# A hybrid decoder layer: all q, k, v projections as plain products ahead of the attention, without sums of x

## The chip, the core and the metric

The kernel runs on one core of one Trainium2 chip. The metric is device time in microseconds (us), the median of several executions. The engines named below are PE (matrix products; PEld is its weight load), DVE, ACT and POOL (element-wise work, each with its own instruction queue, worked off in order) and SP, whose queue issues nearly all DMAs of this kernel.

## What is computed

One decoder layer on x of 2048 rows by 1024 columns, in float32. The parts that matter here:

```python
h = rms_norm(x, g_mix)
z = h @ w_in                                  # 1024 x 3072
u, gb, gc, q, k, v = split(z, 6)              # 512 columns each
y_conv = gb * short_conv(gc * u, conv_w)      # causal, width 3, per channel
q = rms_norm(q per head of 64, g_q) / 8
k = rms_norm(k per head of 64, g_k)
y_attn = dilated_mixture(q, k, v)             # 8 heads, 3 branches (window, dilation)
mix = concat(rms_norm(y_conv), rms_norm(y_attn))
x = x + mix @ w_out
h = rms_norm(x, g_ffn)
x = x + (silu(h @ w_gate) * (h @ w_up)) @ w_down
```

## The kernel before, in words

Every float32 operand of a matrix product is split into a high and a low float16 half, and a product of two operands is three matmuls: high by high, high by low, low by high. The lines are those of the kernel shown at the end of this section. The class that runs is `Fast`; `General` is a fallback that the inputs don't call.

**Stages.** `in_and_conv` normalises x in 16 row tiles (`norm`), transposes them by DMA into `self.x[c]`, c = 0 to 3 with 512 rows each, and runs convolution tile 0 (128 of the 512 channels) on each of them as it arrives (`conv_steps(0, ...)`, matmuls at L191 to L193). Then come the projections: `project(g, c, W)` for four groups g of two heads and four row blocks c. One such call is called a unit in the prediction; there are 16. `attention_pairs` follows: 160 steps of attention (`attn_steps`), and between them steps of `fill`: convolution tiles 1 to 3 and the first part of the output projection, 356 steps. `RATE` is how many fill steps follow an attention step; 24 of them are placed ahead of the first. `out_b` is the rest of the output projection, `ffn` the feed-forward; neither is touched.

**A unit before.** A unit's product is done by Winograd's scheme in blocks of two by two: seven products instead of eight, each of 12 matmuls with 192 columns (L1237), in two halves t. Its left operands are x and four sums of blocks of x. `sums(c)` makes these: POOL adds the halves of x back together (L1134), DVE forms the sums (L1137 to L1140), ACT and DVE split them again (L1144, L1145). Its right operands are made by `operands(g)`: DVE finds the largest weight, ACT scales (L1163), POOL forms the sums (L1175 to L1182), and ACT and DVE split seven blocks (L1171, L1172). The products land in PSUM; ACT copies two of them out (L1247, L1254) and DVE adds the others (L1244). Then a chain follows: ACT squares q and k into the one buffer `row` (L1264) and splits v with DVE (L1267, L1268), DVE reduces (L1274), ACT takes a logarithm and an exponential, DVE does four small operations, POOL scales q and k (L1285) and applies the gain (L1290), ACT and POOL split them into the one buffer `qkhl` (L1294 to L1297), and SP writes it to `d_qk` in memory (L1298).

**Weights for later.** `spill_conv` and `spill_out` prepare the weights of convolution tiles 1 to 3 and of the output projection between the units, by the table `SPILLS`, and write them to memory. Their low halves are formed on DVE (L150, L1334).

**Order and buffers.** A scheduler puts the instructions on each engine's queue; `tc.issue_after(i)` places what follows behind instruction i on i's engine. The sums of x lie in the buffers `qT`, `ka` and `kb`, which the attention needs for q and the two halves of k: `load_pair` fills them by DMA transposes from `d_qk`. `regroup` rearranges q on POOL into `q16`. The attention's pools use the memory that the projection's pools (`tmp`, `fq`) leave.

Of the kernel before, what the change touches and what calls it, by code (L numbers as in the profile page):

```python
# [9 lines left out]
F32 = mybir.dt.float32  # L10
# [8 lines left out]
P = 128  # L19
# [7 lines left out]
HD = 64  # L27
# [983 lines left out]
class Fast(Builder):  # L1011
# [5 lines left out]
    RATE = 2.2  # L1017
# [16 lines left out]
    def in_and_conv(self):  # L1034
# [5 lines left out]
        with ExitStack() as c:  # L1040
# [11 lines left out]
            self.uc = cp.tile([P, 9], F32, name="uc")  # L1052
# [32 lines left out]
            ring = None  # L1085
            n = -1
            for step in self.conv_steps(0, W, before):
# [16 lines left out]
            for g in range(4):  # L1104
                Wg = Wn
                for i in range(4):
                    if g == 0 and i < 2:
                        self.sums(i + 2, s0)
                    if g < 3 and i == 1:
                        Wn = self.operands(g + 1)  # L1110
                    self.project(g, 3 - i if g == 3 else i, Wg)
                    if (g, i) == (0, 2):
                        self.g_out = self.gains(cp, [A["g_conv_out"][0], A["g_attn_out"][0]], "gout", 9)
                    for k in self.SPILLS.get((g, i), ()):
                        self.spill_conv(k // 3, k % 3) if k < 9 else self.spill_out((k - 9) // 2, (k - 9) % 2)
            self.st = dict()

    SPILLS = {(0, 3): (0,), (1, 0): (1, 2), (1, 2): (3,), (1, 3): (4,), (2, 0): (5, 6), (2, 2): (7,), (2, 3): (8,),
              (3, 0): (9, 10), (3, 1): (11, 12)}

    def sums(self, c, s0):
# [5 lines left out]
        Sc = self.sums_of[c] = [pool.tile([P, 2, 2, 4, 256], F16, name=name, bufs=2) for _ in range(2)]  # L1127
        xh, xl = self.x[c]
        for t in range(2):
            y = []  # L1130
            for i in range(2):
                o = slice((2 * t + i) * P, (2 * t + i + 1) * P)
                y.append(self.tmp.tile([P, KC, P], F32, name="t4"))
                nc.gpsimd.tensor_tensor(y[i], xh[:, :, o], xl[:, :, o], op=ALU.add)  # L1134
            a11, a12, a21, a22 = (y[i][:, 4 * k:4 * k + 4] for i in range(2) for k in range(2))
            v = nc.vector
            v.tensor_tensor(a22, a21, a22, op=ALU.add)  # L1137
            v.tensor_tensor(a21, a11, a21, op=ALU.subtract)
            v.tensor_tensor(a11, a22, a11, op=ALU.subtract)
            v.tensor_tensor(a12, a12, a11, op=ALU.subtract)  # L1140
            for i in range(2):
                src = y[i].rearrange("p (a k) t -> p a k t", a=2)
                hi, lo = (Sc[i][:, :, q, :, t * P:(t + 1) * P] for q in range(2))
                nc.scalar.copy(hi, src)  # L1144
                v.tensor_tensor(lo, src, hi, op=ALU.subtract)  # L1145

    def operands(self, g):
# [25 lines left out]
        p = nc.gpsimd  # L1173
        split(0, b11)
# [12 lines left out]
    def qk_constants(self):  # L1187
# [18 lines left out]
        self.vs = [self.fq.tile([P, 4, 2, 2, HD + 1], F16, name=f"vs{i}") for i in range(2)]  # L1206
# [4 lines left out]
    def project(self, g, c, W):  # L1211
# [8 lines left out]
        n = self.row.rearrange("p (j b d) -> p j b d", j=4, b=4)  # L1220
        F = []
        for t in range(2):
            pool, name = ((self.psmm, "mm"), (self.cvx, "cvx"))[self.units % 2]
            self.units += 1
            ps = [pool.tile([P, 512], F32, name=name)[:, 0:192] for _ in range(3)]

            def left(m, q, k):
                if m in (0, 1, 3):
                    i, k0 = {0: (2 * t, 0), 1: (2 * t, 4), 3: (2 * t + 1, 4)}[m]
                    return (xh, xl)[q][:, k0 + k, i * P:(i + 1) * P]  # L1230
                i, a = {5: (0, 0), 2: (0, 1), 6: (1, 0), 4: (1, 1)}[m]
                return Sc[i][:, a, q, k, t * P:(t + 1) * P]

            def product(m):
                for k in range(4):
                    for q, (x, y) in enumerate(((0, 0), (0, 1), (1, 0))):
                        nc.tensor.matmul(ps[self.BANK[m]], lhsT=left(m, x, k), rhs=W[m][:, y, k],  # L1237
                                         start=m in (0, 5, 4) and k == 0 and q == 0, stop=k == 3 and q == 2,
                                         skip_group_check=True)
            f = fq.tile([P, 2, 2, 192], F32, name="f", bufs=3)  # L1240
            F.append(f)

            def plus(o, bank, z):
                nc.vector.scalar_tensor_tensor(o, bank, u, z, op0=ALU.mult, op1=ALU.add)  # L1244
            f11, f12, f21, f22 = (f[:, i, h] for i in range(2) for h in range(2))
            product(0)
            nc.scalar.activation(f21, ps[0], AF.Copy, scale=u)  # L1247
            product(5)
            plus(f12, ps[1], f21)
            product(4)  # L1250
            if (g, c, t) == (0, 0, 0):
                self.squares(3, self.last, self.pstr.tile([P, 4], F32, name="tr"), False)
            product(1)
# [313 lines left out]
    def attention_pairs(self):  # L1567
# [9 lines left out]
        for _ in islice(fill, 24):  # L1577
            pass
# [315 lines left out]
```

## Time and profile before

| | us |
|---|---|
| median of 3 runs | 2207.26 (2206.59 to 2209.81) |
| the profiled execution | 2208.49 |
| its span | 2206.7 |
| PE busy | 2030.8 (92%) |
| DVE busy | 1526.2 (69%) |
| ACT busy | 1047.4 (47%) |
| POOL busy | 726.7 (33%) |
| mean granted TensorE clock | 0.963 |

The profile is of one execution; its own time stands beside its span. Times within it are us from the span's start unless marked ns. A line number is that of kernel and helper, so a helper's line collects all its callers. In the names, `mm`, `cvx`, `s` and `av` are PSUM tiles, `b` is x or a weight in transposed layout. A matmul's own duration overlaps the next one's: the distance of two starts tells the rate. The granted clock is a share of the full TensorE clock. What an engine waited for is inferred from semaphores.

### The profile page before, as it was taken

The numbers are of one execution on the slowest core, as the hardware profiler recorded it, in microseconds if no ns is written. First come the engines' busy times: TensorE is split into PE (matmuls) and PEld (weight loads), VectorE is DVE, ScalarE is ACT, GpSimd is POOL, SyncE is SP. The second block draws the span as 40 slices with busy tenths as digits, with TensorE's granted clock in tenths as the row PEclk, the third lists the DMA queues.
The fourth block names the chain that finished last, engine by engine and source line by source line (L and its number), as shares of the span: only waits on it lengthen the run. The fifth ranks groups of instructions, "written<-read, shape, count | busy, mean of one in ns | idle before, by whom it ended". The sixth has DMA issues, their size and how long they took to land.

```text
span 2206.7 us, 34303 instructions
## 1 busy us (share of the span) xinstructions
PE 2030.8 (92%) x12984; PEld 1115.8 (51%) x12984; DVE 1526.2 (69%) x2893; ACT 1047.4 (47%) x1967; POOL 726.7 (33%) x614
## 2 busy tenths in 40 slices
PE   3868778989999978998999999999999999999998
PEld 1347778946665653443444444444444444444443
DVE  7999885537776886687676666667676676545454
ACT  6445544447775766655333333334333244444341
POOL 2333434433433321122221112112222146555463
PEclk8879789999999998999999999999999999999999
DMA  9524454935867557799522332233222563251442
GB/s 240 138 84 138 158 154 130 192 74 148 180 136 193 167 140 200 244 248 293 161 101 91 101 115 82 91 107 113 90 95 102 210 243 123 77 178 53 130 139 87
DMA packets 460160, 317.00 MB, mean 144 GB/s; under 512 B 255568, under 2 KB 413264, under 8 KB 457808
## 3 DMA queue, kind: packets, MB, share of 16 engines
q1 hardware_dynamic: 442304, 291.56, 46.3%
q10 hardware_dynamic: 17680, 23.16, 2.9%
q8 instruction: 103, 1.69, 0.3%
q14 instruction: 73, 0.60, 0.1%
HBM read 157.96 MB, written 116.85 MB: 125 GB/s over the span
## 4 chain that ended last, share of the span: by engine, by line
PE 46%; issue 5%; DVE 4%; DMA 2%; SPq 2%; ACT 2%; POOL 1%; DVEq 0%; POOLq 0%; ACTq 0%
PE ps L812 28%; PE ps L945 15%; SPq L199 2%; DVE hl L680 1%; PE mm L191 1%; PE mm L192 1%; DVE w L933 1%; PE mm L193 1%; PE ps L191 1%; PE ps L192 0%; PE ps L193 0%; POOL x L952 0%; DMA b<-b 0%; ACT wq L742 0%; DMA wq<-d_a 0%
## 5 line engine op out<-in xcount | busy, mean ns | idle before, releaser
L812 PEld LDWEIGHTS <-w 128*128 128x128 f16 x3696 | 362.2, 98 | 448.0 <-issue 12.7
L812 PE MATMUL ps<-b,w 128*128 128x512 f16 x2112 | 464.8, 381 | 8.7 <-DMA b<-d_h 3.1
L945 PE MATMUL ps<-b,w 128*128 128x512 f16 x1848 | 399.7, 379 | 1.4 <-DVE s L966 0.8
L812 PE MATMUL ps<-hb,w 128*128 128x512 f16 x1584 | 347.1, 379 | 0.0
L945 PEld LDWEIGHTS <-w 128*128 128x128 f16 x1848 | 180.8, 98 | 220.1 <-issue 2.6
L705 POOL TENSOR_TENSOR t<-wq 128x512 f32<-128x512 f32 (+1 forms) x46 | 59.6, 1297 | 407.3 <-issue 231.1
L818 DVE TENSOR_TENSOR s<-ps,s 128x512 f32<-128x512 f32 x220 | 150.1, 683 | 37.1 <-PE ps L812 36.6
L952 POOL TENSOR_TENSOR x<-x,s 128x512 f32<-128x512 f32 x72 | 103.4, 1437 | 170.4 <-DVE s L966 133.1
L1511 DVE TENSOR_TENSOR et<-sm,et 128x512 f16<-128x512 f32 (+1 forms) x160 | 126.3, 807 | 41.8 <-ACT et L1510 40.8
L953 DVE SCALAR_TENSOR_TENSOR x<-ps,a_u,x 128x512 f32<-128x512 f32 x96 | 71.8, 749 | 101.7 <-PE ps L945 75.2
L1505 ACT ACTIVATE sm<-s,bound,kap 128x512 f32<-128x512 f32 (+1 forms) x160 | 116.6, 754 | 53.8 <-DVE s L1503 45.0
L191 PE MATMUL mm<-b,wq 128*128 128x512 f16 x320 | 125.7, 393 | 10.1 <-ACT cg L1360 8.6
L193 PE MATMUL mm<-b,wq 128*128 128x512 f16 x320 | 125.1, 391 | 3.4 <-DVE wq L150 3.4
L1237 PEld LDWEIGHTS <-b 128*128 128x128 f16 x1152 | 107.0, 105 | 40.1 <-issue 37.6
L192 PE MATMUL mm<-b,wq 128*128 128x512 f16 x320 | 125.1, 391 | 0.0
L722 ACT CAST w<-t 128x512 f16<-128x512 f32 x88 | 53.7, 616 | 129.2 <-PE ps L812 81.2
L1503 DVE TENSOR_TENSOR s<-s,mask 128x512 f32<-128x512 f32 (+1 forms) x128 | 80.0, 650 | 34.0 <-PE s L1498 33.6
L1516 PE MATMUL av<-v,et 128*128 128x65 f16 x1800 | 80.8, 195 | 18.2 <-DVE et L1511 16.2
L933 DVE TENSOR_TENSOR w<-t,w 128x512 f16<-128x512 f32 (+1 forms) x96 | 74.5, 794 | 32.9 <-ACT w L932 32.5
L846 ACT ACTIVATE sg<-s,w_un 128x512 f32<-128x512 f32 x66 | 47.3, 719 | 104.5 <-DVE s L818 104.5
L923 ACT ACTIVATE wq<-wq,asf 128x512 f32<-128x512 f32 x88 | 56.6, 711 | 81.5 <-DMA wq<-d_a 78.5
L932 ACT CAST w<-t 128x512 f16<-128x512 f32 (+1 forms) x96 | 53.4, 580 | 85.6 <-PE ps L945 59.8
(323 smaller groups left out, 3878.0 us busy)
## 6 DMA issues: line engine op xcount, KB each, us to landing
d_a<-a ACTq DMA_DIRECT2D x88, 256.0 KB, 2.0
d_wd<-w SPq DMA_DIRECT2D x77, 256.0 KB, 2.0
wq<-d_a SPq DMA_DIRECT2D x64, 256.0 KB, 4.0
b<-d_wd SPq DMA_DIRECT2D x14, 1024.0 KB, 5.7
d_qk<-qkhl SPq DMA_DIRECT2D x16, 768.0 KB, 4.0
d_h<-hl SPq DMA_DIRECT2D x24, 512.0 KB, 3.2
wq<-in_w_gate_dram SPq DMA_DIRECT2D x22, 512.0 KB, 4.7
wq<-in_w_up_dram SPq DMA_DIRECT2D x22, 512.0 KB, 5.0
```

Of the source, the lines that this page charges most:

```text
L191: self.pe = mm(ps, lhsT=lh(k), rhs=rh(k), start=k == ks[0], stop=False)
L192: mm(ps, lhsT=lh(k), rhs=rl(k), start=False, stop=False)
L193: mm(ps, lhsT=ll(k), rhs=rh(k), start=False, stop=k == ks[-1])
L812: nc.tensor.matmul(ps[self.BANK[n]], lhsT=w[:, x, k], rhs=b[:, y, k], start=first and k == 0 and q == 0, stop=k == 3 and q == 2, skip_grou ...
L818: nc.vector.tensor_tensor(t, x, y, op=ALU.add)
L933: nc.vector.tensor_tensor(L[n][:, 1, 0:n_f], src[n], L[n][:, 0, 0:n_f], op=ALU.subtract)
L945: nc.tensor.matmul(ps[self.BANK[n]], lhsT=L[n][:, x, f], rhs=B[n][:, f, y], start=first and f == 0 and q == 0, stop=f == n_f - 1 and q == ...
L952: nc.gpsimd.tensor_tensor(o, o, s_, op=ALU.add)
L1237: nc.tensor.matmul(ps[self.BANK[m]], lhsT=left(m, x, k), rhs=W[m][:, y, k], start=m in (0, 5, 4) and k == 0 and q == 0, stop=k == 3 and q ...
L1505: nc.scalar.activation(e, sp[:, 0:o], AF.Exp, scale=self.kap, bias=self.bound)
L1511: nc.vector.tensor_tensor(et[:, 1], e, et[:, 0], op=ALU.subtract)
L1516: self.pe_av = nc.tensor.matmul(av[:, us.index(u)], lhsT=p_, rhs=v_, start=n_ == 0, stop=n_ == len(ops) - 1)
```

## The change

`PLAIN = 4` makes all four groups plain: a unit is eight products of x and weight blocks, two accumulated on each other in one PSUM tile of 384 columns, so that four tiles a unit are drained, by ACT alone (new L1264). `sums` is not called any more; the branch with seven products stays in the code and isn't taken. `operands` splits four blocks and forms no sums. Square, v and scaling of q and k work on whole units instead of halves. The low halves of the later weights are formed on POOL (new L1344, L1370), three convolution weights share one load and one scale, and the splits are coarser. `SPILLS` and `operands(g + 1)` are placed behind marks of the unit before. `RATE` goes from 2.2 to 1.95, the 24 steps of fill ahead of the attention are placed behind the last projection matmul, and `q16` gets a pool of its own, first in the memory that `tmp` leaves.

```diff
-    RATE = 2.2
+    RATE = 1.95
+    PLAIN = 4
...
+            wanted = [(c, t) for c in range(4) for t in range(2)] if self.PLAIN < 4 else []
...
-                    self.ring = e(tc.tile_pool(name="ring", bufs=9, side="right"))
+                    self.ring = e(tc.tile_pool(name="ring", bufs=8, side="right"))
...
-                elif n in (7, 9):
-                    self.sums(n // 2 - 3, s0)
...
-                    if g == 0 and i < 2:
-                        self.sums(i + 2, s0)
-                    if g < 3 and i == 1:
-                        Wn = self.operands(g + 1)
+                    with ExitStack() as behind:
+                        for m in self.marks:
+                            behind.enter_context(tc.issue_after(m))
...
+                        if g < 3 and i == 1:
+                            Wn = self.operands(g + 1)
...
+                        k = self.SPILLS.get((g, i))
+                        if k is not None:
+                            self.spill_conv(k) if k < 3 else self.spill_out((k - 3) // 2, (k - 3) % 2)
                     self.project(g, 3 - i if g == 3 else i, Wg)
...
-              (3, 0): (9, 10), (3, 1): (11, 12)}
...
+    SPILLS = {(0, 3): 0, (1, 2): 3, (1, 3): 1, (2, 0): 4, (2, 2): 5, (2, 3): 2, (3, 0): 6}
...
+        if g < self.PLAIN:
+            for n, x in ((0, b11), (1, b21), (2, b12), (3, b22)):
+                split(n, x)
+            return W
...
+        f = fq.tile([P, 2, 4, 192], F32, name="f", bufs=2)
...
+        if g < self.PLAIN:
+            for i in range(2):
+                for h in range(2):
+                    ps = self.cvx.tile([P, 512], F32, name="cvx")[:, 0:384]
+                    for k in range(2):
+                        product(ps, lambda t: x_(i, 4 * k, t), W[2 * h + k], k == 0, k == 1)
+                    nc.scalar.activation(block(i, h), ps, AF.Copy, scale=u)
+                last_squares() if i == 0 else None
...
+        for k in range(KC):
+            nc.scalar.activation(raw[:, k], raw[:, k], AF.Copy, scale=sg[:, k:k + 1])
+        for m in range(3):
+            w = self.tmp.tile([P, 2, KC, P], F16, name="t4")
+            src = raw[:, :, m * P:(m + 1) * P]
+            nc.scalar.copy(w[:, 0], src)
+            nc.gpsimd.tensor_tensor(w[:, 1], src, w[:, 0], op=ALU.subtract)
+            nc.sync.dma_start(self.d_wc[j][:, m], w)
...
-                nc.scalar.activation(w[:, 0, k], raw[:, k], AF.Copy, scale=f)
-                nc.vector.scalar_tensor_tensor(w[:, 1, k], raw[:, k], f, w[:, 0, k], op0=ALU.mult, op1=ALU.subtract)
+                nc.scalar.activation(raw[:, k], raw[:, k], AF.Copy, scale=f)
+            nc.scalar.copy(w[:, 0], raw)
+            nc.gpsimd.tensor_tensor(w[:, 1], raw, w[:, 0], op=ALU.subtract)
...
-        t = st["q16"][h] = self.at.tile([P, NT, P], F16, name="q16", bufs=2)
+        t = st["q16"][h] = self.q16.tile([P, NT, P], F16, name="q16", bufs=2)
...
+    def attention(self):
+        with self.tc.tile_pool(name="q16", bufs=1) as self.q16:
+            super().attention()
...
-        for _ in islice(fill, 24):
-            pass
+        with self.tc.issue_after(self.pe.ins):
+            for _ in islice(fill, 24):
+                pass
```

Where instructions stand now. First DVE's queue before, while convolution tile 0 runs (L272 is the low half of a row tile of the normalised x; L1373, L1375 and L1376 are the convolution; L1137 to L1145 make sums of x):

```order
L1145 TENSOR_TENSOR s_840<-t_854,s_840 128x2x4x128
L1382 TENSOR_REDUCE yamax<-cg 128x1
L1137 TENSOR_TENSOR t_927<-t_927 128x512
L272 SCALAR_TENSOR_TENSOR ka<-nx_x,nx_y,ka 128x1024 x2
L1138 TENSOR_TENSOR t_927<-t_925,t_927 128x512
L272 SCALAR_TENSOR_TENSOR kb<-nx_x,nx_y,kb 128x1024 x2
L272 SCALAR_TENSOR_TENSOR ka<-nx_x,nx_y,ka 128x1024
L1139 TENSOR_TENSOR t_925<-t_927,t_925 128x512
L272 SCALAR_TENSOR_TENSOR ka<-nx_x,nx_y,ka 128x1024
L1373 SCALAR_TENSOR_TENSOR cu<-cvx,w_un,cg 128x512
```

And the same place now:

```order
L1418 TENSOR_REDUCE yamax<-cg 128x1
L70 TENSOR_SCALAR nx_v<-nx_ss_663 128x2
L71 RECIPROCAL nx_y<-nx_y 128x2
L72 SCALAR_TENSOR_TENSOR nx_t<-nx_y 128x2
L73 TENSOR_TENSOR nx_t<-nx_t,nx_v 128x2
L74 SCALAR_TENSOR_TENSOR nx_y<-nx_t,nx_y 128x2
L272 SCALAR_TENSOR_TENSOR ka<-nx_x,nx_y,ka 128x1024 x2
L1409 SCALAR_TENSOR_TENSOR cu<-cvx,w_un,cg 128x512
```

The sums are gone from between the norms and the convolution; nothing else comes in. Second, SP's queue before, at the end of the projections (`d_v` and `d_qk` are writes of a unit, the transposes are `load_pair`):

```order
L199 DMA_TRANSPOSE ka<-d_qk_132 128x2x512 x3
L199 DMA_TRANSPOSE ka<-d_qk_133 128x2x512 x2
L1271 DMA d_v_64<-vs_1073 128x4x130 x2
L199 DMA_TRANSPOSE ka<-d_qk_133 128x2x512 x2
L199 DMA_TRANSPOSE qT<-d_qk_132 128x2x512
L1298 DMA d_qk_135<-qkhl 128x4x768
L199 DMA_TRANSPOSE qT<-d_qk_132 128x2x512 x3
```

Now these transposes stand with the first units of groups 0 and 1; this is SP's queue from the first unit's `d_qk` on (L1162 loads the weights of a later group):

```order
L1323 DMA d_qk_132<-qkhl 128x4x768
L199 DMA_TRANSPOSE qT<-d_qk_132 128x2x512
L1162 DMA wq<-in_w_in_dram 128x8x128 x3
L1301 DMA d_v_61<-vs_1009 128x4x130 x2
L199 DMA_TRANSPOSE ka<-d_qk_132 128x2x512
L199 DMA_TRANSPOSE kb<-d_qk_132 128x2x512
L1323 DMA d_qk_132<-qkhl 128x4x768
```

The first pair's q and k are transposed unit by unit, each right behind the write that it reads. Third, PE's queue at the last projection matmuls, before (L191 to L193 are convolution tile 1, from `fill`):

```order
L1237 MATMUL cvx<-w,s_841 128x192
L191 LDWEIGHTS wq
L191 MATMUL mm<-b_114,wq 128x512
L192 LDWEIGHTS wq
L192 MATMUL mm<-b_115,wq 128x512
```

And now:

```order
L1249 MATMUL cvx<-w,b_114 128x192
L1249 LDWEIGHTS b_115
L1249 MATMUL cvx<-w,b_115 128x192
L191 LDWEIGHTS wq
L191 MATMUL mm<-b_114,wq 128x512
```

Before, 46 matmuls of tile 1 stand between the last projections; now all 3072 projection matmuls come first, then 66 of tile 1 and the first score matmuls. Behind the last attention step 42 matmuls of fill are left, 30 of them in one piece; before there are none.

More of the change, by code (lines that the diff above doesn't have):

```diff
@@ L1128, in sums @@
         xh, xl = self.x[c]
[L1129 to L1145, printed above, removed]
+        y = []
@@ L1205, in qk_constants @@
         nc.gpsimd.memset(self.qkhl[:, :, 4:6, 1], 0.0)
-        self.vs = [self.fq.tile([P, 4, 2, 2, HD + 1], F16, name=f"vs{i}") for i in range(2)]
+        self.vs = [self.fq.tile([P, 2, 4, 2, HD + 1], F16, name=f"vs{i}") for i in range(2)]
         for t in self.vs:
@@ L1219, in project, with x_ @@
         vs = self.vs[c % 2]
-        n = self.row.rearrange("p (j b d) -> p j b d", j=4, b=4)
-        F = []
-        for t in range(2):
+        n = self.row.rearrange("p (h j b d) -> p h j b d", h=2, j=4, b=2)
+        f = fq.tile([P, 2, 4, 192], F32, name="f", bufs=2)
+        block = lambda i, h: f[:, h, 2 * i:2 * i + 2].rearrange("p t c -> p (t c)")
+        def x_(i, k0, t):
+            o = slice((t + 2 * i) * P, (t + 2 * i + 1) * P)
+            return lambda q, k: (xh, xl)[q][:, k0 + k, o]
@@ new lines, in s_, with product @@
+        def s_(i, a, t):
+            return lambda q, k: Sc[i][:, a, q, k, t * P:(t + 1) * P]
+        def product(ps, left, w, start, stop):
+            for t in range(2):
+                lh = left(t)
+                with self.tc.issue_after(first.ins) if t else nullcontext():
+                    for k in range(4):
+                        for q, (x, y) in enumerate(((0, 0), (0, 1), (1, 0))):
+                            self.pe = nc.tensor.matmul(ps[:, 192 * t:192 * (t + 1)], lhsT=lh(x, k), rhs=w[:, y, k],
+                                                       start=start and t + k + q == 0, stop=stop and k == 3 and q == 2,
+                                                       skip_group_check=True)
+                            if t + k + q == 0:
+                                first = self.pe
@@ new lines, in last_squares @@
+        def last_squares():
+            if (g, c) == (0, 0):
+                self.squares(3, self.last, self.pstr.tile([P, 4], F32, name="tr"), False)
+        if g < self.PLAIN:
+            for i in range(2):
+                for h in range(2):
[4 more added lines that the diff above has]
+                last_squares() if i == 0 else None
+        else:
@@ L1223, in project @@
             pool, name = ((self.psmm, "mm"), (self.cvx, "cvx"))[self.units % 2]
             self.units += 1
[L1225 to L1241, printed above, removed]
+            ps = [pool.tile([P, 512], F32, name=name)[:, 0:384] for _ in range(3)]
@@ L1247, in project @@
[L1247 to L1253, printed above, removed]
-            nc.scalar.activation(f11, ps[0], AF.Copy, scale=u)
-            product(6)
-            plus(f22, ps[1], f21)
-            plus(f22, ps[2], f22)
-            product(3)
-            plus(f21, ps[1], f21)
```

112 lines of the change are left out of this document (71 added, 41 removed).

## The prediction

> **What bounds the kernel now.** I read the table of windows first, cut where the trace changes its character: convolution tile 0 to 132.7 us, the projections to 451.1, the hand-over to 473.4, the attention to 823.9, a pause to 836.9, then the second half of the output projection and the feed-forward. The columns are the stretch, its length, then busy time and instructions of PE, PEld, DVE, ACT and POOL, the granted TensorE clock, the DMA share and GB/s.
>
> ```profile
> 25.00:100.00 75.00, 55.97 (x256) 27.14 (x256) 72.28 (x105) 43.03 (x70) 26.75 (x11) 0.88 0.66 161
> 100.00:132.70 32.70, 21.87 (x88) 10.33 (x89) 28.61 (x40) 13.47 (x20) 13.31 (x7) 0.76 0.48 139
> 132.70:451.10 318.40, 261.13 (x2734) 246.57 (x2734) 238.06 (x620) 155.74 (x361) 127.37 (x135) 0.89 0.56 146
> 451.10:473.40 22.30, 13.68 (x55) 5.64 (x53) 5.17 (x10) 5.04 (x12) 14.29 (x16) 0.77 0.29 87
> 473.40:823.90 350.50, 327.33 (x3640) 216.31 (x3638) 265.48 (x459) 248.02 (x473) 115.24 (x92) 0.97 0.61 150
> 823.90:836.90 13.00, 0.02 (x1) 0.00 (x0) 8.44 (x41) 5.94 (x16) 1.34 (x6) 0.50 0.71 211
> 1106.00:2206.70 1100.70, 1092.27 (x5057) 494.71 (x5056) 697.06 (x1184) 413.71 (x730) 371.72 (x290) 1.00 0.34 116
> ```
>
> From 1106 us on PE is busy 99% at clock 1.00, and the change does not touch that code: those 1100.7 us only shift. What can move lies before 837 us. Until 100 us DVE is full (72.3 of 75); in the projections PE is busy 261 of 318 us and its clock is 0.89. What a clean stream costs there is in the timeline of PE late in that stage (start, length, line):
>
> ```profile
> 427.51 1.15 PE L1237 MATMUL cvx<-w,qT 128*128 128x192 f16 x12
> 428.50 1.15 PE L1237 MATMUL mm<-w,b 128*128 128x192 f16 x12
> ```
>
> Twelve projection matmuls start in 0.99 us, 82.5 ns each. The 2688 of this stage would take 221.8 us; the other 46 of its 2734 belong to the convolution that comes next (9.9 us at 215.6 ns, below). So 318.4 - 231.7 = 86.7 us are pauses and slow clock. What the pauses ended on is in PE's waits over the stage (total, times, longest):
>
> ```profile
> PE cvx L1237 <- ACT f L1247: 19.7, 9, 4.7
> PE mm L1237 <- DVE f L1244: 15.1, 8, 4.1
> PE mm L1237 <- ACT w L1171: 11.9, 3, 6.7
> ```
>
> Evacuations by ACT and DVE, and the weight split. They wait in queues that the next rows fill (the view of a line: count, shortest/median/longest ns, first and last start).
>
> ```profile
> L1137 DVE TENSOR_TENSOR t<-t x8: 641/1458/2587, 34.1 to 133.5; 128x512 f32<-128x512 f32 x8
> L1138 DVE TENSOR_TENSOR t<-t,t x8: 671/682/2297, 34.9 to 137.2; 128x512 f32<-128x512 f32 x8
> L1145 DVE TENSOR_TENSOR s<-t,s x4: 1214/1218/1221, 45.0 to 62.8; 128x1024 f16<-128x1024 f32 x4
> L1134 POOL TENSOR_TENSOR t<-b,b x16: 2111/2287/3103, 26.5 to 129.2; 128x1024 f32<-128x1024 f16 x16
> L1244 DVE SCALAR_TENSOR_TENSOR f<-mm,uq,f x80: 375/414/419, 154.7 to 435.7; 128x192 f32<-128x192 f32 x80
> L1172 DVE TENSOR_TENSOR w<-wq,w x28: 918/951/2314, 135.2 to 389.6; 128x768 f16<-128x768 f32 x28
> L150 DVE SCALAR_TENSOR_TENSOR t<-t,w_sg,t x72: 307/345/1351, 155.4 to 263.2; 128x128 f16<-128x128 f32 x72
> ```
>
> **Products and what they cost on PE.** Seven products of 12 matmuls become eight: 192 instead of 168 matmuls for each (group, tile), which I call a unit, so 3072 in all, 384 more. At 82.5 ns that is +31.7 us, and the whole stream is 253.4 us. The change loses if nothing else gives way.
>
> **What leaves DVE.** The sums: eight half tiles, each with 1.46 + 3 x 0.68 (L1138 stands for the three like it) + 2 x 1.22 = 5.9 us, 48 us. The 160 evacuations by L1244 (80 on `mm`, 80 on `cvx`), 66 us: the plain products accumulate in PSUM and ACT alone drains them. Twelve of the 28 operand splits, 11 us. The 72 low halves at L150 go to POOL, 25 us. That is 150 us; a unit keeps on DVE one wide low half of v, one reduction and four small operations.
>
> **Start of the projections, -26 us.** The timeline of PE shows the first matmul of tile 0's fourth chunk and the first projection.
>
> ```profile
> 100.53 0.61 PE L191 MATMUL cvx<-b,wq 128*128 128x512 f16 x1 [8.24 <-DMA b<-kb]
> ...
> 132.71 0.32 PE L1237 MATMUL mm<-w,b 128*128 128x192 f16 x1 [4.92 <-ACT w L1171]
> ```
>
> PE waited 8.2 us for a transpose whose input had stood behind sums on DVE. Without them PE gets there at about 92, less some us for smaller pauses before, say 89. The chunk's 72 matmuls take 15.5 us at full clock: 105. The operands of group 0 are loaded right behind those transposes, and their scale factors no longer queue behind the sums of tiles 1 to 3; they are ready at about the same time. I take 107 for the first projection. The ends are 132.7 (the operands are as late as now) and 100 (PE never waits).
>
> **The units, -57.6 us.** From 132.7 to 451.1 now; then 253.4 us of stream plus 7 for pauses, 260.8. The choice is the clock. The stage's row says 0.89, and at 0.89 the stream would be 285 us; the feed-forward, where PE hardly pauses, runs at 1.00. I take 1.00, because the pauses go. [...] The other engines' shares come from rows of the same kinds:
>
> ```profile
> L1163 ACT ACTIVATE wq<-wq,w_sg x32: 597/600/615, 127.8 to 252.6; 128x384 f32<-128x384 f32 x32
> L1264 ACT ACTIVATE row<-f x32: 613/629/632, 167.3 to 451.9; 128x512 f32<-128x512 f32 x32
> L1274 DVE TENSOR_REDUCE qk_ss<-row x16: 1205/1210/1220, 176.2 to 452.6; 128x16 f32<-128x1024 f32 x16
> L1285 POOL TENSOR_TENSOR row<-f,qkr_y x32: 1037/1042/2024, 180.1 to 456.3; 128x512 f32<-128x512 f32 x32
> L1290 POOL TENSOR_TENSOR row<-row,gk x16: 1262/1268/1386, 182.2 to 457.4; 128x512 f32<-128x512 f32 x16
> L1296 POOL TENSOR_TENSOR qkhl<-row,qkhl x32: 662/671/1387, 183.7 to 459.2; 128x256 f16<-128x256 f32 x32
> L1295 ACT CAST qkhl<-row x32: 602/614/624, 189.5 to 459.2; 128x512 f16<-128x512 f32 x32
> ```
>
> Four drains (2.4), the double-width square (1.3), v, two small functions and four copies like L1295 (an estimate of 3.6): 7.3 us of a unit's 15.8. Ten units also carry weight work of at most 8 us (eight scalings of 0.6, three or four casts of about 1). POOL has 2.1 + 1.3 + 4 x 0.67 = 6 us, and in seven units two or three splits at L1134's 2.29. Both fit, ACT narrowly (15.3 of 15.8), and four PSUM banks of 4 us each cover a late drain. The wide operations are at worst neutral here: their sizes are the old ones added up.
>
> **The hand-over, +9.9 and -8 us.** The 46 convolution matmuls that stood among the last units now stand behind them (+9.9). In return they cover the last unit's tail:
>
> ```profile
> 451.14 0.38 PE L192 MATMUL mm<-b,wq 128*128 128x512 f16 x1
> ...
> 456.53 0.38 PE L193 MATMUL mm<-b,wq 128*128 128x512 f16 x1
> 465.54 0.58 PE L191 MATMUL mm<-b,wq 128*128 128x512 f16 x1 [8.62 <-ACT cg L1360]
> ```
>
> The first two rows are 25 matmuls apart, 215.6 ns each. PE then stood 8.6 us because the buffer of the convolution was free only 14.4 us after the last projection (the stage's end, 451.1); 66 matmuls and more now fill 14.2 us of that, and the clock stays up (0.77 now).
>
> The q, k transposes move on SP's queue from behind the last units to right behind each d_qk write. One such write takes 4.0 us to land, one transpose about 1.4 us of the queue (DMA issues; the line's view):
>
> ```profile
> d_qk<-qkhl SPq DMA_DIRECT2D x16, 768.0 KB, 4.0
> L199 SPq DMA_TRANSPOSE kb<-d_qk x16: 1245/1380/3673, 401.0 to 662.4; - x16
> ```
>
> SP waits for the landing with loads of weights and v writes queued behind; the next unit's v write and the weights of the group after are theirs to delay. A unit's SP work of some 10 us fits in 15.8, and the weights are wanted a group later, so I cost it at nothing; where it isn't covered, it is part of the rival below. What is late next is the load of v, which lies behind the last d_qk: I leave 3 us.
>
> **The attention, +3 and -7 us.** It is 160 steps, and fill is 356 steps with 960 matmuls. With 24 of them ahead, at 2.2 a step fill ends nine steps early. PE's largest wait in the attention, and its end in the timeline:
>
> ```profile
> PE av L1516 <- DVE et L1511: 16.2, 18, 2.3
> ```
>
> ```profile
> 822.64 1.28 PE L1516 MATMUL av<-v,et 128*128 128x65 f16 x20 [0.41 <-DVE et L1511]
> 836.92 0.61 PE L191 MATMUL mm<-b,b 128*128 128x512 f16 x1 [13.00 <-ACT b L585]
> ```
>
> PE is busy 327 of 350 us, so the attention is bound by PE and work taken out of it shortens it. At 1.95 some 42 matmuls (9 us) go behind the last step; 30 of them stand together there, 6.5 us of the 13.0 that PE waited for the load of `ya`. Total PE work is the same, so the gain is the pause filled, -7 (ends 0 and -13). With less fill a step has 2.0 us instead of 2.16 of PE; DVE has 1.6 of that now (265 by 160, with fill's part), so pauses like L1511's grow: +3 (ends 0 and +12).
>
> **The sum.** -25.7 - 57.6 + 9.9 - 8 + 3 - 7 = -85. The profiled execution took 2208.5 us, its span 2206.7 and 1.8 around it; the median shown is 2207.3, so I forecast 2122.
>
> **Rivals.** One: ACT's queue holds the drains up. In the ten units with weight work ACT needs 15.3 of 15.8 us, and each wait for POOL's half of the chain comes on top; at 19 us for such a unit +27 us, 2149. Against it: four banks, and six light units to recover in. Two: the weight loads become the limit.
>
> ```profile
> L1237 PEld LDWEIGHTS <-b x1152: 95/98/291, 127.4 to 450.0; 128*128 128x128 f16 x192
> ```
>
> One load is busy 98 ns, longer than the 82.5 of a matmul. One behind the other 3072 take 301 us, +48, 2170; against it, 82.5 ns is measured with a load for every matmul. [...] Three, slower than before: the chain through the single `row` buffer. The next unit's square waits in ACT's queue until POOL has done with the last one: 1.3 + 1.2 + about 1.2 of small steps + 3.3 + 4 = 11 us, in 15.8. If the weight work (8 us on ACT, 6.9 on POOL) stands inside that chain it is 25.8, and ten units make +95 us: 2217. It decides from 21.6 us a unit over all sixteen. For it: POOL's and DVE's queues do hold both kinds of work; against: scheduled apart, they overlap. That the change doesn't do what it says I see only for the rate: if the attention keeps its pace by DVE, the loss is inside the ends above.
>
> **How the numbers follow.** About 0.2%, 4.4 us, is what a measurement of this kernel can tell from no change. Chances: the forecast 0.74 (2095 to 2140, from the ends of the start, pauses and pace), the drains 0.14, the loads 0.04, the row chain 0.04, and 0.04 for still faster. The range 2095 to 2160 takes the forecast's ends and most of rival one. Faster 0.95; within 0.2% 0.01; slower 0.04.
>
> **What would show it.** Right: first projection near 107 us, 3072 matmuls at 82.5 ns and clock near 1.00 with under 15 us of pauses, first score matmul some 17 us after the last projection, a pause under 7 us ahead of the second output half, and everything from there moved by one amount. Wrong: a unit longer than 17 us, with PE waiting for the drains (ACT `f`); a first projection after 120; score matmuls that wait for q or k; or a step of the attention still at 2.19 us.

## The result and the profile after

The changed kernel takes 2119.8 us (median of 4 runs, 2118.9 to 2121.7), the kernel before 2208.1 beside it (2206.6 to 2209.8): a ratio of 0.960, 95% interval 0.958 to 0.962. The forecast was 2122.0, the range 2095 to 2160. The profiled span is 2118.5 us, 88.2 less than before, at a mean granted clock of 0.989.

The table of windows of the changed kernel, cut at the same places as before: the stretch, its length, busy time and instructions of PE, PEld, DVE, ACT and POOL, the granted clock, the DMA share and GB/s.

```profile
25.00:83.00 58.00, 50.51 (x255) 25.61 (x255) 33.04 (x75) 33.33 (x59) 0.00 (x0) 1.00 0.97 204
83.00:104.10 21.10, 18.34 (x81) 8.34 (x81) 9.14 (x20) 7.15 (x14) 0.00 (x0) 0.92 0.45 110
104.10:370.00 265.90, 257.31 (x3082) 256.26 (x3081) 124.47 (x259) 152.36 (x280) 126.80 (x114) 0.99 0.72 179
370.00:384.20 14.20, 14.20 (x68) 6.42 (x67) 4.52 (x12) 6.33 (x14) 9.01 (x9) 1.00 0.41 89
384.20:728.80 344.60, 323.42 (x3629) 212.72 (x3627) 264.08 (x457) 247.58 (x476) 116.90 (x94) 0.99 0.63 160
728.80:737.80 9.00, 6.65 (x30) 2.83 (x30) 6.76 (x34) 4.31 (x13) 1.55 (x6) 1.00 0.70 243
737.80:1018.00 280.20, 262.91 (x1183) 117.13 (x1184) 204.59 (x383) 148.66 (x263) 56.44 (x45) 0.96 0.82 222
1018.00:2118.50 1100.50, 1090.49 (x5047) 492.87 (x5045) 691.00 (x1176) 412.91 (x730) 371.67 (x290) 1.00 0.35 116
```

DVE is no longer full in tile 0 (33 of 58 us). The projections have 384 matmuls more than before and take 52.5 us less. DVE's work in them falls from 238 us to 124. The hand-over is PE without a pause (14.2 of 14.2). The last row has its old length; what was won lies ahead of it.

The timeline of PE in the projections shows the stream and where it breaks (start, length, line, count, idle before and what ended it):

```profile
104.51 8.00 PE L1249 MATMUL cvx<-w,b 128*128 128x192 f16 x95 [0.15 <-DVE w L1180]
...
113.18 150.64 PE L1249 MATMUL cvx<-w,b 128*128 128x192 f16 x1824
264.42 8.08 PE L1249 MATMUL cvx<-w,b 128*128 128x192 f16 x96 [0.60 <-ACT f L1264]
277.25 33.87 PE L1249 MATMUL cvx<-w,b 128*128 128x192 f16 x384 [4.75 <-ACT f L1264]
312.60 31.95 PE L1249 MATMUL cvx<-w,b 128*128 128x192 f16 x384 [1.48 <-ACT f L1264]
346.15 23.92 PE L1249 MATMUL cvx<-w,b 128*128 128x192 f16 x288 [1.60 <-ACT f L1264]
```

1824 matmuls run on end, 82.5 ns apart. Nearly ten units pass like that, 15.8 us each. Then come four pauses, all behind a drain on ACT, 8.4 us together. After the longest the 384 matmuls take 33.9 us instead of 31.7: the granted clock was 0.50 in the first 3.75 us behind it, so that this pause cost some 2 us beyond its length. The pauses of 1.5 and 1.6 us cost no more than they last (384 matmuls in 31.95 us; the granted clock was 1.00 in the 3.75 us behind each).

The same stages before and after, forecast and measured, as differences of their starts (us):

| step | forecast | measured | from |
|---|---|---|---|
| first projection | -25.7 | -28.6 | 132.7 to 104.1 |
| the units | -57.6 | -52.6 | 318.4 to 265.8 |
| last projection to first score | +1.9 | -8.0 | 22.3 to 14.3 |
| first score to the end | -4 | +1.0 | 1733.3 to 1734.3 |
| sum | -85.4 | -88.2 | |

Where the last row's gain went is seen behind the attention. The pause ahead of the second output half shrank as forecast (timeline of PE; before it was 13.0 us):

```profile
729.83 0.39 PE L193 MATMUL mm<-b,b 128*128 128x512 f16 x1 [1.07 <-DVE b L586]
...
737.81 0.39 PE L191 MATMUL ps<-b,b 128*128 128x512 f16 x1 [1.33 <-ACT b L585]
```

But PE's waits in the output stage that follows grew. First the changed kernel, then the one before (total, times, longest):

```profile
PE mm L191 <- DVE qT L599: 7.0, 1, 7.0
PE ps L812 <- DMA b<-d_h: 5.2, 2, 4.9
```

```profile
PE mm L191 <- DVE qT L599: 2.4, 1, 2.4
PE ps L812 <- DMA b<-d_h: 3.1, 1, 3.1
```

The 7.0 is a drain on DVE that stands behind other work in DVE's queue (its timeline there):

```profile
817.09 0.17 DVE L70 TENSOR_SCALAR opr_v<-op_ss 128x2 f32<-128x2 f32 x1 [3.50 <-ACT b L634]
...
819.57 0.69 DVE L672 TENSOR_TENSOR b<-ka 128x512 f32<-128x512 f32 x1 [1.40 <-ACT ka L669]
...
822.71 1.22 DVE L680 TENSOR_TENSOR hl<-ka,hl 128x1024 f16<-128x1024 f32 x1
823.85 0.68 DVE L675 TENSOR_TENSOR b<-ka,b 128x512 f32<-128x512 f32 x1
824.45 0.74 DVE L599 SCALAR_TENSOR_TENSOR qT<-mm,rau,qT 128x512 f32<-128x512 f32 x1
```

DVE waits for ACT twice and forms sums and low halves before it comes to the drain. A PE that arrives earlier only waits longer for it: 4.6 us of the filled pause, and 2.1 us at `d_h`, were given back.

### The profile page after: what moved, and what is told of

Its sections match the earlier page's. It is cut to its first block, busy times and chain, and to the rows that moved or that the text cites. A ratio compares the mean times of both kernels' runs of the same rounds, so it can differ in the third digit from the quotient of the medians.

```text
span 2118.5 us, 34421 instructions
## 1 busy us (share of the span) xinstructions
PE 2024.2 (96%) x13368; PEld 1122.3 (53%) x13368; DVE 1354.1 (64%) x2487; ACT 1031.3 (49%) x1876; POOL 686.1 (32%) x574
## 5 line engine op out<-in xcount | busy, mean ns | idle before, releaser
L1249 PE MATMUL cvx<-w,b 128*128 128x192 f16 x3072 | 256.7, 247 | 8.6 <-ACT f L1264 8.4
L1249 PEld LDWEIGHTS <-b 128*128 128x128 f16 x3072 | 255.4, 98 | 9.9 <-issue 9.3
L191 PE MATMUL mm<-b,wq 128*128 128x512 f16 x320 | 123.3, 385 | 0.0
L192 PE MATMUL mm<-b,wq 128*128 128x512 f16 x320 | 123.1, 385 | 0.0
L193 PE MATMUL mm<-b,wq 128*128 128x512 f16 x320 | 123.0, 384 | 0.0
L96 DVE TENSOR_REDUCE vm_a<-wq 128x1 f32<-128x2048 f32 (+2 forms) x32 | 77.3, 2416 | 52.0 <-DMA wq<-in_w_up_dram 24.4
L1552 PE MATMUL av<-v,et 128*128 128x65 f16 x1800 | 81.5, 194 | 19.1 <-DVE et L1547 12.8
L933 DVE TENSOR_TENSOR w<-t,w 128x512 f16<-128x512 f32 (+1 forms) x96 | 75.4, 802 | 36.7 <-ACT w L932 36.3
```

The costliest lines, as they stand in the source:

```text
L191: self.pe = mm(ps, lhsT=lh(k), rhs=rh(k), start=k == ks[0], stop=False)
L192: mm(ps, lhsT=lh(k), rhs=rl(k), start=False, stop=False)
L193: mm(ps, lhsT=ll(k), rhs=rh(k), start=False, stop=k == ks[-1])
L1249: self.pe = nc.tensor.matmul(ps[:, 192 * t:192 * (t + 1)], lhsT=lh(x, k), rhs=w[:, y, k], start=start and t + k + q == 0, stop=stop and k ...
L1552: self.pe_av = nc.tensor.matmul(av[:, us.index(u)], lhsT=p_, rhs=v_, start=n_ == 0, stop=n_ == len(ops) - 1)
```

## The experiments

All are compared with the kernel before, run beside them (2206 to 2208 us): behind the median time stand the ratio to it and the ratio's 95% interval. Where a step is read against the changed kernel, its 2119.8 us is meant.

**1. The plain products alone**, put into the kernel before (sums not called, the product branch replaced):

```diff
-            product(0)
-            nc.scalar.activation(f21, ps[0], AF.Copy, scale=u)
...
+            for i in range(2):
+                for h in range(2):
+                    bank = self.cvx.tile([P, 512], F32, name="cvx")[:, 0:192]
...
+                    nc.scalar.activation(f[:, i, h], bank, AF.Copy, scale=u)
...
-                elif n in (7, 9):
-                    self.sums(n // 2 - 3, s0)
```

> The kernel before with the eight plain products alone: no sums of x, four operand splits, eight narrow drains a unit on ACT; the low halves of the later weights stay on DVE, rate 2.2, the order of the queues and the narrow operations stay. Theory (DVE was in the way by the sums and the evacuations): the first projection comes near 107 us, the stream of 3072 matmuls takes 253 us plus some 25 us of pauses behind the weight splits still on DVE, the rest is as before: 2208 - 26 - 35 = 2147 us (2130 to 2165). Rival (the gain comes from the placement behind marks, the wide operations and POOL's weight splits; 384 more matmuls only cost): 2208 + 31.7 and no more than 20 off the start, 2190 us or more.

Measured: 2160.9 us, 0.979 (0.977 to 0.981). The windows' row of its projections, and PE's timeline with the first and the last stretch of them:

```profile
104.40:405.40 301.00, 269.12 (x3099) 263.39 (x3099) 159.37 (x449) 167.48 (x412) 94.01 (x119) 0.95 0.62 163
```

```profile
104.43 0.24 PE L1222 MATMUL cvx<-w,b 128*128 128x192 f16 x1 [0.37 <-ACT w L1167]
...
306.71 98.93 PE L1222 MATMUL cvx<-w,b 128*128 128x192 f16 x1176 [2.93 <-ACT f L1225]
```

The start is there in full (104.4). Of the units only 17.4 us are (318.4 to 301.0). Once the weight work is over, 1176 matmuls run without a pause; before that they don't. The total lies in the theory's range, near its upper end, but the units give 17.4 us where the theory has 35. What takes them on from 301.0 to 265.8 us is something else, and DVE, busy 159 of 301 us, is not short of time.

**2. Two groups by seven products** (`PLAIN = 2`):

```diff
-    PLAIN = 4
+    PLAIN = 2
```

> The changed kernel with two groups plain and two by seven products (the branch that it keeps): 2880 matmuls of 192 columns instead of 3072, sums of x half a tile at a time among the first eight units, DVE adding up the products in the last eight. Theory (the sums hurt by where they stood, ahead of the first projection): the stream stays clean, 15.8 us less of it, some 10 us back at the operands of groups 2 and 3, 2114 us (2104 to 2130). Rival (products that DVE has to take out and add cannot feed PE cleanly): the last eight units fall back to the 19.3 us each that they took before (308.5 by 16) from 16.6, +22 us, 2142 us (2135 to 2155).

Measured: 2173.0 us, 0.985 (0.983 to 0.987). The rival's side, and dearer than it said. The projections take 299.8 us for 2880 matmuls; PE's waits there, the three longest:

```profile
PE mm L1249 <- ACT f L1279: 11.2, 2, 10.4
PE mm L1249 <- DVE f L1275: 10.7, 6, 3.2
PE mm L1249 <- ACT w L1179: 9.0, 3, 7.8
```

192 matmuls less save 15.8 us, and yet the stage is 34.0 us longer than the changed kernel's: the drains of the seven products, their weights and the sums cost three times what they save. The wait for `w` may owe something to the ring of eight buffers, where the kernel before had nine; that wasn't separated.

**3. The sums of x back, unused**:

```diff
-            wanted = [(c, t) for c in range(4) for t in range(2)] if self.PLAIN < 4 else []
+            wanted = [(c, t) for c in range(4) for t in range(2)]
...
-                elif self.PLAIN == 1 and n in (8, 10):
+                elif n in (8, 10):
```

> The changed kernel with the sums of x computed again, half a tile each at two steps of convolution tile 0 and six among the first units, and read by nobody: their work alone is added. Theory (DVE delayed the start of the projections, and has room within the units: 124 us busy of 266): the first projection comes some 6 to 12 us later, the units keep their pace, 2120 + 10 = 2130 us (2122 to 2136). Rival one (the sums are hidden wherever they stand; what cost before was the evacuation): no change, 2120. Rival two (48 us of DVE and 37 us of POOL stand in the queues of a unit's chain): the first units grow by over 3 us each, 2145 us or more.

Measured: 2157.0 us, 0.977 (0.975 to 0.979). Rival two. PE's timeline:

```profile
108.14 0.32 PE L1249 MATMUL cvx<-w,b 128*128 128x192 f16 x1 [3.24 <-ACT w L1179]
112.08 12.16 PE L1249 MATMUL cvx<-w,b 128*128 128x192 f16 x113 [3.62 <-DVE w L1180]
...
227.77 26.78 PE L1249 MATMUL cvx<-w,b 128*128 128x192 f16 x288 [5.18 <-ACT f L1264]
...
303.63 30.36 PE L1249 MATMUL cvx<-w,b 128*128 128x192 f16 x336 [5.35 <-ACT f L1264]
...
347.54 58.31 PE L1249 MATMUL cvx<-w,b 128*128 128x192 f16 x672 [9.27 <-ACT f L1264]
```

The first matmul comes 4.0 us later, and PE waits some 3.5 us more right behind it, for DVE's low halves of the weights; together that is what I gave the start. The rest, 28 us, is paid in the later units, but not in the second to the sixth, where most of the sums stand: these run clean, and the seventh is the first of them to pause. I read it so: the work puts the chain behind PE, and PE notices only when no buffer is left. The sums also take turns with the later weights in the buffers `t4`, so it is not shown that the time of DVE and POOL alone is the price.

**4. The square four times**:

```diff
-        nc.scalar.activation(nv.rearrange("p x b d -> p x (b d)"), fi[:, :, 0:128], AF.Square)
+        for _ in range(4):
+            nc.scalar.activation(nv.rearrange("p x b d -> p x (b d)"), fi[:, :, 0:128], AF.Square)
```

> The changed kernel with the square of q and k computed four times over (the same values written again): 3.2 us more of ACT a unit, right behind the last drain, in the chain through the buffer row. Theory (four PSUM tiles and a chain of 11 us in a unit of 16 cover it): PE's waits for the drains grow from 8.4 us to some 15, 2126 us (2119 to 2134). Rival (ACT's queue holds the drains up in the units with weight work, where it has 15.3 of 15.8 us): +3.2 us in ten units or more, 2152 us or more.

Measured: 2164.7 us, 0.980 (0.978 to 0.982), 45 us over the changed kernel. My theory falls. PE's waits up to the first scores:

```profile
PE cvx L1249 <- ACT f L1264: 28.4, 5, 9.4
PE s L1535 <- ACT sm L1542: 17.0, 1, 17.0
```

Here too the first ten units stay at their pace. Then PE pauses 28 us (the units take 289.4 us, 23.6 more), and 17 us more stand at the first scores, where PE waits for ACT; I read it as ACT still busy with the last units. Over the sixteen units there was no cover for 3.2 us each.

**5. The reduction four times**, the same on DVE:

```diff
-        nc.vector.tensor_reduce(ss, nv.rearrange("p x b d -> p (x b) d"), axis=AX.X, op=ALU.add)
+        for _ in range(4):
+            nc.vector.tensor_reduce(ss, nv.rearrange("p x b d -> p (x b) d"), axis=AX.X, op=ALU.add)
```

> The changed kernel with the sum of squares of q and k reduced four times over on DVE (the same values written again): 3.7 us more in the chain of each unit, no work more for ACT or POOL, and DVE has room (124 us busy of 266, 55 more). Theory A and theory B (the chain's length, or ACT's waiting in order, makes the lag): much like the four squares, +25 to +50 us, 2145 to 2170. Rival (ACT's own busy time is what was short with the four squares): 2120 to 2126.

Measured: 2163.9 us, 0.980 (0.978 to 0.982), 44 us over. Half of it stands in the units (287.5 us, 21.7 more), most of the rest at the first scores:

```profile
PE s L1535 <- ACT sm L1542: 23.9, 5, 20.8
```

The price is the same without a microsecond of work more on ACT or POOL, and on the engine that had half its time free: what the two have in common is the length of the chain, not an engine's busy time. Each also holds its own engine's queue for that much longer; these two runs don't separate that from the chain.

**6. Two buffers for `row` and `qkhl`**:

```diff
-        n = self.row.rearrange("p (h j b d) -> p h j b d", h=2, j=4, b=2)
+        n = fq.tile([P, D], F32, name="row", bufs=2).rearrange("p (h j b d) -> p h j b d", h=2, j=4, b=2)
...
-        hl = self.qkhl
+        hl = self.hls[c % 2]
```

> The changed kernel with two buffers each for row and for qkhl, used in turn. Theory A (the units run up a lag through the one buffer row: the next square waits until POOL has split the last unit): the four pauses of 8.4 us in all and the slow clock behind them go, the projections take 255 to 258 us instead of 265.7, 2110 us (2106 to 2114). Theory B (ACT works off its queue in order, and a waiting copy or scaling holds up the drains behind it whatever the buffers): no change, 2120 us (2116 to 2124).

Measured: 2128.4 us, 0.964 (0.962 to 0.966). Theory A fails: in the eleventh and the thirteenth unit, where the changed kernel pauses 4.75 and 1.48 us, two longer pauses stand (PE's timeline). The projections take 271.5 us. The profile is of the fastest of the five runs (2122.7 us); the median is out of theory B's range too.

```profile
278.35 34.16 PE L1250 MATMUL cvx<-w,b 128*128 128x192 f16 x384 [6.40 <-ACT f L1265]
317.82 29.27 PE L1250 MATMUL cvx<-w,b 128*128 128x192 f16 x336 [5.30 <-ACT f L1265]
```

So the two single buffers don't make the pauses. What theory B named is left, ACT's queue worked off in order; that it does is not shown by this run alone.

**7. The later weights spread out**:

```diff
-    SPILLS = {(0, 3): 0, (1, 2): 3, (1, 3): 1, (2, 0): 4, (2, 2): 5, (2, 3): 2, (3, 0): 6}
+    SPILLS = {(0, 2): 0, (1, 0): 3, (1, 2): 1, (2, 0): 4, (2, 2): 2, (3, 0): 5, (3, 1): 6}
```

> The changed kernel with another table for the later weights: units 2, 4, 6, 8, 10, 12 and 13 instead of 3, 6, 7, 8, 10, 11 and 12, so that between two units with weight work there is mostly one without (the operands stay at 1, 5 and 9). Theory (weight work in consecutive units adds up to the lag that PE pays from the tenth unit on): the pauses fall from 8.4 us to under 3, the projections to some 257 us, 2111 us (2107 to 2116). Rival (each weight work costs its own stall, wherever it stands): no change, 2120 (2116 to 2125).

Measured: 2131.0 us, 0.966 (0.964 to 0.968), 11 us slower than the changed kernel, and outside both ranges. The three longest pauses are 3.6, 3.6 and 4.1 us, in units 6, 10 and 14 (counted from 0, as in the table); the units take 275.1 us in all. With the operands in units 1, 5 and 9 this table still leaves neighbours with weight work, 4 to 6, 8 to 10, 12 and 13, and each of these pauses stands at the end of such a row or right behind it. So the table does not bring about what the theory asks for and leaves it untested, and the rival is not shown either: most of the weight works cost no pause of their own.

**8. No weights ahead of the operands of unit 9**:

```diff
-    SPILLS = {(0, 3): 0, (1, 2): 3, (1, 3): 1, (2, 0): 4, (2, 2): 5, (2, 3): 2, (3, 0): 6}
+    SPILLS = {(0, 2): 3, (0, 3): 0, (1, 2): 4, (1, 3): 1, (2, 2): 5, (2, 3): 2, (3, 0): 6}
```

> The changed kernel with the later weights in units 2, 3, 6, 7, 10, 11 and 12 (output, convolution, output, convolution, output, convolution, output): the only change is that unit 8, ahead of the operands in unit 9, has none. Theory (the stall of 4.75 us at unit 10 arises where the operands follow weights of the output projection: their scaling on ACT waits for DVE, whose search for the largest weight waits in turn): the stall goes, the units take some 258 us instead of 265.7, 2113 us (2108 to 2117). Rival (it arises from the two weight works of units 9 and 10): no change, 2120 us (2117 to 2125).

Measured: 2126.6 us, 0.963 (0.962 to 0.964). The stall moves rather than goes: 3.7 us in unit 6, 3.7 in unit 10 and 2.3 in unit 14, and the units take 272.7 us. The first projection is also 2.5 us later (106.6). The table changes more than unit 8: it moves a work into unit 2 and shifts another to unit 6, so the theory is not tested alone.

**9. Two of four drains on DVE**:

```diff
-                    nc.scalar.activation(block(i, h), ps, AF.Copy, scale=u)
+                    if h:
+                        nc.vector.tensor_scalar_mul(block(i, h), ps, u)
+                    else:
+                        nc.scalar.activation(block(i, h), ps, AF.Copy, scale=u)
```

> The changed kernel with two of a unit's four drains on DVE, whose queue has 124 us of work in 266, instead of ACT. Theory (the drains that PE waits for stand in ACT's queue behind scalings and copies that wait for DVE and POOL): every second drain passes them, and 1.1 us a unit less of ACT work; the pauses fall from 8.4 us to some 3, 2113 us (2108 to 2118). Rival (DVE's queue waits too, for the square and for 3.3 us of the search for the largest weight): the drains on DVE are late instead, 2120 to 2135 us.

Measured: 2127.2 us, 0.963 (0.962 to 0.964). The rival: nine pauses of 0.5 to 1.9 us, now behind DVE as often as behind ACT, and 268.6 us for the units. Either queue waits. Only 2.8 us of the loss are in the units; 5.0 lie behind the first score, where the edit changes no instruction.

**10. The convolution ahead of the attention, free**:

```diff
-        with self.tc.issue_after(self.pe.ins):
-            for _ in islice(fill, 24):
-                pass
+        for _ in islice(fill, 24):
+            pass
```

> The changed kernel with the 24 steps of convolution ahead of the attention free to be placed where the scheduler likes, as before. By the prediction's term (the convolution covers the tail of the last unit, 8 us): PE waits again between the projections and the scores, the same work otherwise, 2128 us (2124 to 2132). Rival (some 46 matmuls stand among the last units and fill PE's pauses there, and PE meets the attention with less fill behind it): no change, 2120 us (2116 to 2123).

Measured: 2117.6 us (2116.4 to 2121.1), 0.959 (0.958 to 0.961): no difference. The scheduler puts these matmuls behind the projections without being told; from the last projection to the first score it is 14.3 us again. So the placement behind the last projection is worth nothing here, and leaving it out is no shown gain either, since the runs of both kernels overlap.

**11. Rate 2.2**:

```diff
-    RATE = 1.95
+    RATE = 2.2
```

> The changed kernel with 2.2 fill steps an attention step, as before. By the prediction's term the pause of some 13 us ahead of the second output half comes back and costs 7 us: 2127 us (2123 to 2132). Rival (what the filled pause gained is given back in the output stage, where PE then waits 7.0 us for DVE at L599 and 5.2 for d_h): the attention ends some 9 us later, the stage behind it is some 5 to 9 us shorter, 2121 us (2118 to 2123).

Measured: 2142.1 us, 0.971 (0.969 to 0.973): 22 us slower, and neither theory. The row of its attention (the one at 1.95 stands above):

```profile
384.70:752.40 367.70, 338.80 (x3671) 220.81 (x3669) 275.06 (x465) 252.88 (x477) 119.47 (x96) 0.96 0.61 150
```

23.1 us longer. 42 more matmuls of fill are 9.1 us (at 215.6 ns). PE's busy time grew by 15.4, so 6.3 are slow clock (0.96 instead of 0.99), and 7.7 are idle. PE's waits for the split scores, at 2.2 and then at 1.95:

```profile
PE av L1552 <- DVE et L1547: 21.1, 19, 3.5
```

```profile
PE av L1552 <- DVE et L1547: 12.8, 17, 2.7
```

In this kernel less fill a step goes with fewer of these waits. But the rate of 2.2 does not make them by itself. The kernel of experiment 1 runs at 2.2 too, with as many matmuls in its attention (3671); it takes 353.3 us there, at clock 0.99, and its waits for the split scores are

```profile
PE av L1482 <- DVE et L1477: 12.7, 23, 1.4
```

What makes the same rate some 14 us dearer in the changed kernel was not found.

**12. Without the marks**:

```diff
-                        for m in self.marks:
+                        for m in ():
```

> The changed kernel without the marks: operands and later weights may be placed ahead of the reduction, v and the gain of the unit before, as in the kernel before; products, wide operations, POOL's low halves, table and rate stay. Theory (of the 36.7 us between the profiled runs of the kernel before with plain products alone and the changed kernel, most is the place in DVE's queue: there the reduction of q and k stood behind a search for the largest weight that waited 5.3 us for a load, and ACT stood 6.2 us for it with the next drains behind): the projections take 290 us or more, 2145 us (2138 to 2160). Rival (the 35 us come from fewer and wider operations and the low halves on POOL): the projections take under 275 us, 2120 to 2130 us.

Measured: 2164.5 us, 0.981 (0.979 to 0.982). The theory holds, and more than all of the difference that it set out from is there (36.9 us, 2157.16 to 2120.25; the expectation says 36.7): 44.7 over the changed kernel, 308.1 us for the projections. The rival falls with it: the wide operations and POOL's low halves without the marks do not beat experiment 1 (308.1 us to 301.0 for the projections). The marks on narrow operations were not run. ACT's two largest waits in them, without the marks and then in the changed kernel:

```profile
ACT qkr_t L1305 <- DVE qk_ss L1304: 35.5, 11, 9.4
ACT qkhl L1319 <- POOL row L1312: 34.7, 11, 8.3
```

```profile
ACT qkhl L1319 <- POOL row L1312: 20.1, 6, 3.9
ACT qkr_t L1305 <- DVE qk_ss L1304: 17.7, 14, 7.9
```

One of these waits at its source, DVE's timeline without the marks and ACT's right behind it:

```profile
162.72 3.35 DVE L96 TENSOR_REDUCE vm_a<-wq 128x1 f32<-128x3072 f32 x1 [2.39 <-DMA wq<-in_w_in_dram]
165.99 1.21 DVE L96 TENSOR_REDUCE vm_a<-t 128x1 f32<-128x1024 f32 x1
167.12 1.21 DVE L1304 TENSOR_REDUCE qk_ss<-row 128x16 f32<-128x1024 f32 x1
```

```profile
168.36 0.31 ACT L1305 ACTIVATE qkr_t<-qk_ss,lnb 128x16 f32<-128x16 f32 x1 [6.68 <-DVE qk_ss L1304]
```

The search for the largest weight (L96) waits for its load, runs 4.6 us in two pieces, and only then comes the reduction on which ACT, and behind ACT the next drains, wait. Its input was there before: ACT, which makes it, stood idle from 161.7 us on.

## Why the prediction was right, and where it was not

**The start** was right in size. 107 was forecast, 104.1 came, and the plain products alone give 104.4, with the later weights and the queues' order left as they were. How this divides between the sums of x and the operand splits is not separated: two half tiles of sums put back there cost 4.0 us, and 3.5 behind the first matmul.

**The units.** Their saving was forecast 5.0 us too large, and most of it came from a cause that had no term. The prediction took 150 us off DVE and concluded that the pauses go. Experiment 12 has all that work off DVE and experiment 1 most of it, and the units still take 308 and 301 us. What brings them to 266 is the marks. They set the weight work behind the chain's own operations in the queues; without them the stage loses 42 of the 52.6 us that it gained. The mechanism stood in the text as rival three, the weight work inside the chain, with 0.04. "Scheduled apart, they overlap" was said against it. They are scheduled apart because of an edit that the sum passed over. The rival had the place right; the price without the marks is 45 us, not 95. That the delay runs through the one buffer `row`, as the rival had it, is not shown: experiment 6 gave it a second buffer only with the marks in place.

**The cover** was overrated: "both fit" and "four PSUM banks of 4 us each cover a late drain". Two experiments that stretch the chain by 3.2 and 3.7 us a unit cost 45 and 44 us, about half of it in the units and the rest up to and at the first scores. The chain's queues run behind PE in the units with weight work, and several units go by before PE stops. Rival one, at 0.14, had the place of these waits, the drains on ACT, but its reason, ACT's 15.3 of 15.8 us, is not what the runs show: experiment 5 adds nothing to ACT and costs the same.

**The stream** was right: 1824 matmuls 82.5 ns apart at clock 1.00, each with a load of 98 ns by the median (L1249 on PEld, as many loads as matmuls in that stretch), so the loads overlap and rival two is out. The clock of the whole stage was 0.99, with 8.4 us of pauses left in it, where 1.00 was taken and 0.89 stood before.

**The hand-over** was mis-sized: +1.9 in the sum, -8.0 measured. The sum added 46 matmuls to a stretch that already held 55. In the changed kernel 68 stand there, and some 30 more (6.5 us) moved behind the first score, into the next stretch. The forecast of 17 us to the first score, in the same text, was near the 14.3 measured and did not agree with the sum. The wait for the load of v, for which 3 us were left without a term in the sum, is 0.7.

**The attention and what follows** came out at +1.0 instead of -4, of which the 30 matmuls from the hand-over are 6.5. The pause was filled as the -7 had it: of 13.0 us, 2.4 are left. But 6.7 us were given back in the output stage. That pauses grow with less fill, the +3, has the wrong sign in this kernel: at 1.95 the waits for the split scores are 12.8 us instead of 21.1, the clock of the attention is 0.99 instead of 0.96, and the lower rate is worth 22 us in it, not 7. Yet nothing like 22 us was won, because 20 were lost beside it: 2.2 in the changed kernel is 20.3 slower in this part than 2.2 was before (1753.6 to 1733.3). The plain products alone, at 2.2 and with the same 30 matmuls moved, lose only 6.4 there (1739.8 in experiment 1). The other 14 came with the remaining edits, and stand in the attention itself; which of them it is (the pool of `q16`, the wide operations, the marks, or the order that they give) is open. "Everything from there moved by one amount" was wrong as well: 95.1 us at the last attention matmul (823.9 to 728.8), 88.2 at the end.

So the total was met within 3 us with errors, measured less forecast, of -2.9 (start), +5.0 (units), -9.9 (hand-over) and +5.0 (attention and after). Of the last two, 6.5 us are the same work on the other side of a border. That the rest cancels is luck, and so is that the 22 us of the rate and the 20 lost beside them nearly do. The forecast held the range through the large terms, the start and the clean stream; that the stream runs clean is owed to the marks.

Open is also what the last 8.4 us of pauses need. Four attempts (6 to 9) moved or stretched them and came out 7 to 11 us slower. Each edit also changes the order of queues elsewhere, so that differences of this size need not come from the edit's own mechanism. A third buffer for `f` wasn't tried. Of the kernels run, none is shown to beat the changed one.

## What to carry to other kernels

In the units of this kernel, work taken off an engine paid only where its queue then served the critical operation earlier: look at what stands ahead of that operation in each in-order queue, not at the engine's share. Give every ordering edit a term of its own, even when it adds no instruction. A stream that runs clean for ten units can still be at its limit; stretch its chain by a few microseconds to learn how much cover it has.

## What the hardware showed beyond that

Two small DVE operations ran until a POOL operation beside them ended. The timeline of DVE in the changed kernel, and of POOL at the same time:

```profile
265.39 0.17 DVE L1308 SCALAR_TENSOR_TENSOR qkr_t<-qkr_y 128x16 f32<-128x16 f32 x1
265.47 0.20 DVE L101 STREAM_TRANSPOSE vm_t<-vm_a 128x32 f32<-128x32 f32 x1
265.60 1.98 DVE L1309 TENSOR_TENSOR qkr_t<-qkr_t,qk_ss 128x16 f32<-128x16 f32 x1
...
268.01 1.83 DVE L106 TENSOR_TENSOR vm_r<-vm_r 32x1 f32<-32x1 f32 x1
```

```profile
265.38 2.17 POOL L1370 TENSOR_TENSOR t<-t,t 128x1024 f16<-128x1024 f32 x1 [13.71 <-DMA d_qk<-qkhl]
267.93 1.90 POOL L1312 TENSOR_TENSOR row<-f,qkr_y 128x1024 f32<-128x1024 f32 x1 [0.38 <-DVE qkr_y L1310]
```

Two operations of 0.15 to 0.2 us took 1.98 and 1.83 and ended within 0.03 us of POOL's. The transposition (L101) ran beside POOL's in 0.20; L1308, which began within 0.01 us of POOL's start, took its usual 0.17. In the units' chain it is rare: of the 14 operations of L1309 in the projections the other 13 took 0.13 to 0.18 us. In the search for the largest weight it is not: of the 22 of L105 and L106 there nine took 1.66 to 1.89 us, L106's in the rows above among them, and each ended within 0.02 us of an operation of L1312. What makes an operation wait like that was not shown. The first of the two above stands in a unit's chain and took 1.8 us more than the others of L1309, beside a low half that the change moved from DVE to POOL (L1370).
